# A two-layer decoder trunk on one core: second FFN preparation without GpSimd sums, a written order for its last tiles, and two smaller moves

## The chip, the core and the metric

The kernel runs on one core of a Trainium2 chip. A core has TensorE (PE, matrix products and transposes into PSUM), VectorE (DVE), ScalarE (ACT), GpSimd (POOL) and SyncE (SP, which here issues the DMA transfers). Each engine takes its own instructions in order; waits between engines go by semaphores. The metric is the device time of one execution in microseconds, lower is better.

## The reference

Two residual layers work on x of 1024 tokens x 1024 features in float32. Layer 0 mixes tokens by gMLP and by dilated attention (8 heads, three dilations), layer 1 by chunked gated linear attention (GLA). Each layer then has a gated FFN with a causal convolution of width 3 and 2816 hidden features. Cut to what matters here:

```python
for layer in range(2):
    h = rms_norm(x, norm_mix_g[layer])
    x = x + (even_mixer if layer % 2 == 0 else gla_mixer)(h, ...)   # ends in cat @ w_out
    h = rms_norm(x, norm_ffn_g[layer])
    x = x + conv_ffn(h, ...)

def conv_ffn(h, w_gate, w_up, conv_w, conv_b, w_down):
    g = causal_dwconv(h @ w_gate, conv_w, conv_b)
    return (silu(g) * (h @ w_up)) @ w_down
# attention: the branches of different dilation are weighted by a softmax over their log-denominators and summed
```

## The kernel before, in words

A matrix product takes each float32 operand in two parts: a rounded one (`split`: ScalarE casts it, L108) and the remainder (VectorE subtracts, L109), and does three passes over them. In the rows the parts carry their tile's name, such as `hq` (turned activations), `wo` (out projection), `da` and `dw` (FFN down). A scheduler lists the instructions of each engine in an order of its own, by its own estimates; `tc.keep_in_program_order(ins)` pins an instruction behind the pinned one traced ahead of it on its engine.

Attention runs head pair by head pair (four pairs). A slot of the main loop takes one tile n = 0..7 of a pair: scores, softmax rows, transposes into `pP`, a copy to `pT` (L828, VectorE for even tiles, ScalarE for odd ones), and products into `po`. While pair p runs, the near and the far branch of pair p - 1 are combined (`combine`, `combined`, L941 to L968): group 0 (four token tiles) in slot 4, group 1 in slot 5. A combination takes small operations on `cM`, `cE`, `cD`, one multiplication of `ot` on GpSimd, one of `on` on VectorE (both L964), and an addition (L966).

After the mixer comes the out projection, in column halves: `out_first` makes columns 0 to 511 of all tiles, `out_second` columns 512 to 1023 and, tile by tile, the norm and the transposes for the FFN. The FFN products are done as seven half-size products (p = 1 to 7) on sums of blocks. `first_sides` makes the weight sums for the first feature block while `out_first` runs: for "g" and for "u" it loads two tiles `qg`/`qu`, makes four sums `qS` (p = 5, 6, 7, 3; L249, GpSimd), splits them into `qw` and stores them. `out_second` takes the tiles in the order 0, 4, 1, 5, 2, 3, 6, 7; a tile n >= 4 is combined with tile n - 4 (`second`): four sums `tf..0` to `tf..3`, of which the parts go to `T3[0]`, `T3[1]`, `T3[2]` (rows `T`) and `hq`. The sums t3 and t4 are on GpSimd, except t3 of tile 7. `out_half` runs TensorE's 24 matmuls of a tile (`po1n`, L210) with the transposes of an earlier tile (`pt`, L164) put between them. Tile 7's part (`norm_last`) is handed to `ffn_up` as `norm_end` and stands among its first products `pgB`, `puB`, `puA`, `pgA`; the ones on `T3` are `pgC`, `puC`.

`ffn_down` takes seven products in chunks of two feature pairs: for each, SyncE loads activations `ar` and weights `wr`, which are split into `da` and `dw`; the products go to banks `pdB`, `pdC` (p = 1), `pdO`, `pdP`, `pdQ` (p = 2) and so on. Ahead of all chunks it loads the residual rows `xs[n]` (rows `xr`, eight of 512 KB, L408).

Of the kernel before, what the change touches and what calls it, by code (L numbers as in the profile page):

```python
# [10 lines left out]
F32 = mybir.dt.float32  # L11
# [51 lines left out]
def trunk(ctx: ExitStack, tc: tile.TileContext, a, out):  # L63
# [174 lines left out]
    def first_sides(l, pool, bufs):  # L238

        for kind in "gu":  # L240
# [6 lines left out]
            def summed(p, x, y, op):  # L247
                made[p] = pool.tile([P, 512], F32, tag="qS", bufs=2, name=f"qS{l}{kind}{p}")
                G.tensor_tensor(made[p], x, y, op=op)  # L249
                return made[p]  # L250
# [155 lines left out]
    def ffn_down(l, ps, pool, xs, final):  # L406
        for n in range(NT):
            Q.dma_start(xs[n], xd[l][n])  # L408

# [18 lines left out]
        for p, b, half, c in ((1, "B", 0, 0), (2, "O", 0, 0), (6, "B", 1, 0), (5, "O", 1, 1), (7, "B", 1, 1),  # L428
# [3 lines left out]
            for i, fps in enumerate(CHUNKS):  # L432
                late = p == 4 and fps[0] >= FP // 2 * 2 - TAIL
                both = sides(p, i, pool, tag="tail", bufs=2 * TAIL + 2) if late else sides(p, i)
                if late:
# [62 lines left out]
    def out_second(l, w, x_in, T3, ps, pool):  # L498
# [17 lines left out]

        def second(n, turn, k, b):
            last = n == 7
            gains = gT[:, 0:KD:2, None].to_broadcast([P, 4, P])

            def put(g, pt):
                if last and g == 0:
                    V.tensor_tensor(b[:, g], pt, gains, op=ALU.mult)
                    return
                for j in range(4):
                    A.mul(b[:, g, j, :], pt[:, j, :], gT[:, 2 * j + g : 2 * j + g + 1])

            turn(put, True)
            E = V if last else G
            t1, t2, t3, t4 = (F4(pool.tile([P, 512], F32, tag="S", bufs=4, name=f"tf{n}{i}")) for i in range(4))  # L530
            V.tensor_tensor(t1, b[:, 0], k[:, 0], op=ALU.subtract)
            split(place(T3[0], n), t1)
            V.tensor_tensor(t2, b[:, 1], t1, op=ALU.subtract)
            split(place(T3[1], n), t2)
            E.tensor_tensor(t3, b[:, 1], b[:, 0], op=ALU.subtract)
            split(place(T3[2], n), t3)
            G.tensor_tensor(t4, k[:, 1], t2, op=ALU.subtract)
# [3 lines left out]
        def norm_last(n, xt, ps, junk, h):  # L541

            early = squares(f"{n}a", xt[:, :512], junk[:, :512])
            G.tensor_scalar(early, early, EPS * D, None, op0=ALU.add)

            def rest():
                r = squares(f"{n}b", xt[:, 512:], junk[:, 512:])
                G.tensor_scalar(r, r, early, 1.0 / D, op0=ALU.add, op1=ALU.mult)
                G.tensor_tensor(r, r, mhalf[:, :1], op=ALU.pow)
                for _, c in HALVES:  # L550
                    V.tensor_scalar(h[:, c], xt[:, c], r, None, op0=ALU.mult)
# [969 lines left out]
```

## Time and profile before

| | |
|---|---|
| median of three runs | 2138.92 us (2138.76 to 2140.26) |
| the profiled execution | 2138.33 us |
| its span | 2136.6 us |
| TensorE busy | 2115.9 us (99% of the span), 20.7 us idle |
| VectorE, ScalarE, GpSimd busy | 71%, 48%, 24% |
| granted TensorE clock | 1.000 |
| DMA | 358.66 MB, mean 168 GB/s |

A timeline row gives the start and the length in us, the engine, the line, the operation, the tile written and those read (buffer numbers left out), and in brackets the idle time of the engine just before and what ended it. An "x11" joins instructions that follow one another. A row of the view of waits gives the engine and tile that waited, what it waited for, the total in us, how often, and the longest. The busy time of TensorE includes matmuls that follow one another more slowly than usual.

### The profile page before, as it was taken

The numbers are of one execution on the slowest core, as the hardware profiler recorded it, in microseconds if no ns is written. First come the engines' busy times: TensorE is split into PE (matmuls) and PEld (weight loads), VectorE is DVE, ScalarE is ACT, GpSimd is POOL, SyncE is SP. The second block draws the span as 40 slices with busy tenths as digits, with TensorE's granted clock in tenths as the row PEclk, the third lists the DMA queues.
The fourth block names the chain that finished last, engine by engine and source line by source line (L and its number), as shares of the span: only waits on it lengthen the run. The fifth ranks groups of instructions, "written<-read, shape, count | busy, mean of one in ns | idle before, by whom it ended". The sixth has DMA issues, their size and how long they took to land.

```text
span 2136.6 us, 29596 instructions
## 1 busy us (share of the span) xinstructions
PE 2115.9 (99%) x10380; PEld 1794.7 (84%) x10380; DVE 1514.2 (71%) x2398; ACT 1035.0 (48%) x2008; POOL 523.4 (24%) x553
## 2 busy tenths in 40 slices
PE   8999999999999999999999999999999999999999
PEld 8999988878888888878899888888788888888887
DVE  7466664586878888565576877686788889785554
ACT  7555563365444444344454455545544444444443
POOL 6344311133425344000010011032334334220000
PEclk9999999999999999999999999999999999999999
DMA  7122314854444444755553232396554544458564
GB/s 261 45 74 64 105 45 154 297 198 161 156 150 158 167 163 160 263 212 206 208 176 109 82 103 99 113 329 224 201 171 155 176 147 155 163 172 297 210 221 163
DMA packets 161908, 358.66 MB, mean 168 GB/s; under 512 B 17584, under 2 KB 55216, under 8 KB 161376
## 3 DMA queue, kind: packets, MB, share of 16 engines
q1 hardware_dynamic: 161616, 356.66, 49.2%
q8 instruction: 81, 1.33, 0.3%
q14 instruction: 67, 0.55, 0.1%
q10 hardware_dynamic: 144, 0.13, 0.0%
HBM read 244.20 MB, written 111.74 MB: 167 GB/s over the span
## 4 chain that ended last, share of the span: by engine, by line
PE 72%; DVE 3%; ACT 2%; DMA 1%; issue 1%; SPq 0%; POOL 0%; DVEq 0%; ACTq 0%; POOLq 0%
PE puB L312 11%; PE pgB L312 11%; PE pgC L312 6%; PE puC L312 6%; PE pdB L422 5%; PE pdC L422 5%; PE pv L210 4%; PE pdO L422 4%; PE po L210 3%; PE puA L312 3%; PE pgA L312 3%; PE pdP L422 2%; PE pdQ L422 2%; PE pBq L1212 2%; PE pBr L1212 1%
## 5 line engine op out<-in xcount | busy, mean ns | idle before, releaser
L109 DVE TENSOR_TENSOR da<-ar,da 128x512 fp32r<-128x512 f32 x154 | 106.3, 690 | 154.6 <-ACT da L108 154.4
L108 ACT CAST da<-ar 128x512 fp32r<-128x512 f32 x154 | 95.9, 623 | 211.7 <-PE pdC L422 96.4
L210 PE MATMUL po<-wo,hq 128*128 128x512 f32 x768 | 183.1, 394 | 0.5 <-DVE hq L109 0.4
L210 PEld LDWEIGHTS po<-wo,hq 128*128 128x128 f32 x768 | 142.0, 188 | 30.3 <-DVE hq L109 1.1
L210 PE MATMUL pv<-wv,hq 128*128 128x512 f32 (+2 forms) x768 | 142.3, 341 | 0.0
L422 PE MATMUL pdB<-dw,da 128*128 128x512 f32 x528 | 135.4, 390 | 1.3 <-ACT dw L108 1.3
L422 PE MATMUL pdC<-dw,da 128*128 128x512 f32 x528 | 135.1, 390 | 0.0
L210 PEld LDWEIGHTS pv<-wv,hq 128*128 128x128 f32 x768 | 118.6, 189 | 14.4
L210 PE MATMUL pj<-wq,hq 128*128 128x384 f32 x576 | 120.6, 343 | 0.0
L422 PEld LDWEIGHTS pdB<-dw,da 128*128 128x128 f32 x528 | 98.8, 188 | 22.3 <-ACT dw L108 1.7
L422 PEld LDWEIGHTS pdC<-dw,da 128*128 128x128 f32 x528 | 99.1, 188 | 20.5
L278 POOL TENSOR_TENSOR S1g<-rg 128x512 f32<-128x512 f32 x20 | 29.6, 1481 | 352.0 <-DMA wsd<-D 183.3
L109 DVE TENSOR_TENSOR dw<-wr,dw 128x512 fp32r<-128x512 f32 x154 | 105.8, 687 | 10.5 <-ACT dw L108 9.9
L422 PE MATMUL pdO<-dw,da 128*128 128x512 f32 x396 | 102.2, 389 | 0.2 <-DVE dw L109 0.2
L108 ACT CAST dw<-wr 128x512 fp32r<-128x512 f32 x154 | 95.0, 617 | 11.6 <-DMA wr<-in_w_dn 8.2
L210 PEld LDWEIGHTS pj<-wq,hq 128*128 128x128 f32 x576 | 97.0, 188 | 0.0
L422 PEld LDWEIGHTS pdO<-dw,da 128*128 128x128 f32 x396 | 74.3, 188 | 15.9 <-DVE dw L109 0.6
L153 POOL TENSOR_SCALAR rn<-ssq 128x1 f32<-128x1 f32 x22 | 6.1, 278 | 325.9 <-ACT h L173 244.9
L343 DVE SCALAR_TENSOR_TENSOR t<-g,cw,t 128x1022 f32<-128x1022 f32 x44 | 73.8, 1676 | 0.1
L342 DVE SCALAR_TENSOR_TENSOR t<-g,cw,t 128x1023 f32<-128x1023 f32 x44 | 59.3, 1349 | 16.3 <-ACT t L341 16.3
L327 DVE TENSOR_TENSOR g<-g,s1g 128x512 f32<-128x512 f32 x22 | 15.2, 693 | 78.1 <-ACT s1g L326 78.1
L278 POOL TENSOR_TENSOR S4u<-ru,S2u 128x512 f32<-128x512 f32 x20 | 48.9, 2444 | 54.6 <-DVE wg2p L109 9.7
(1084 smaller groups left out, 5436.1 us busy)
## 6 DMA issues: line engine op xcount, KB each, us to landing
ar<-actd SPq DMA_DIRECT2D x70, 512.0 KB, 3.6
rd<-in_w_down SPq DMA_DIRECT2D x44, 512.0 KB, 3.7
wsd<-D SPq DMA_DIRECT2D x88, 256.0 KB, 2.4
rg<-in_w_gate SPq DMA_DIRECT2D x40, 512.0 KB, 3.7
ru<-in_w_up SPq DMA_DIRECT2D x40, 512.0 KB, 4.7
wr<-wsd SPq DMA_DIRECT2D x40, 512.0 KB, 4.4
actd<-t SPq DMA_DIRECT2D x66, 256.0 KB, 2.2
wr<-in_w_dn SPq DMA_DIRECT2D x30, 512.0 KB, 5.0
```

Of the source, the lines that this page charges most:

```text
L108: (hi or A.copy)(dst[0], src)
L109: (lo or V.tensor_sub)(dst[1], src, f32(dst[0]))
L153: G.tensor_scalar(r, ssq, 1.0 / n, EPS, op0=ALU.mult, op1=ALU.add)
L210: yield T.matmul(o, L[i], R[jj][:, sl], start=(k == 0 and (ii, jj) == PASSES[0]), stop=(k == nk - 1 and (ii, jj) == PASSES[-1]))
L278: G.tensor_tensor(sums[name], x, y, op=op)
L312: mm = T.matmul(o, L[ii][:, j * P : j * P + P], right[p][:, jj, j, :], skip_group_check=more, start=(not more and j == 0 and (ii, jj) == P ...
L327: V.tensor_add(C22, C22, s1)
L342: V.scalar_tensor_tensor(t[:, 1:], g[:, : S - 1], w(1), t[:, 1:], op0=ALU.mult, op1=ALU.add)
L343: V.scalar_tensor_tensor(t[:, 2:], g[:, : S - 2], w(0), t[:, 2:], op0=ALU.mult, op1=ALU.add)
L422: T.matmul(o, L[ii][:, t * P : t * P + P], R[jj], skip_group_check=more, start=start and not more and (ii, jj) == PASSES[0], stop=stop and ...
L1212: T.matmul(o, L[ii][:, j * P : j * P + P], right[p][:, jj, j, :], skip_group_check=more, start=(not more and j == 0 and (ii, jj) == PASSES ...
```

## The change

Four edits: `combine` for group 1 runs in slot 6 instead of slot 5; the sums of `first_sides` are on VectorE; `out_second` has all its sums on VectorE and its last tiles (2, 3, 6, 7) written out with pinned instructions; and `ffn_down` issues the residual loads between the chunks of p = 1 and p = 2, each before the chunk's own products.

```diff
@@ -246,7 +246,7 @@
 
             def summed(p, x, y, op):
                 made[p] = pool.tile([P, 512], F32, tag="qS", bufs=2, name=f"qS{l}{kind}{p}")
-                G.tensor_tensor(made[p], x, y, op=op)
+                V.tensor_tensor(made[p], x, y, op=op)
                 return made[p]
 
             for p in (5, 6, 7, 3, 4, 1, 2):
@@ -404,9 +404,6 @@
 
 
     def ffn_down(l, ps, pool, xs, final):
-        for n in range(NT):
-            Q.dma_start(xs[n], xd[l][n])
-
         def sides(p, c, pool=None, **tag):
 
             k = len(CHUNKS[c])
@@ -432,6 +429,8 @@
             for i, fps in enumerate(CHUNKS):
                 late = p == 4 and fps[0] >= FP // 2 * 2 - TAIL
                 both = sides(p, i, pool, tag="tail", bufs=2 * TAIL + 2) if late else sides(p, i)
+                if p < 3 and i < 4:
+                    tc.keep_in_program_order(Q.dma_start(xs[4 * p - 4 + i], xd[l][4 * p - 4 + i]))
                 if late:
                     tail += both
                     continue
@@ -514,65 +513,112 @@
 
             turn(put, True)
 
+        pin = tc.keep_in_program_order
+
+        def gained(g, pt, b, hold=lambda ins: ins):
+            for j in range(4):
+                hold(A.mul(b[:, g, j, :], pt[:, j, :], gT[:, 2 * j + g : 2 * j + g + 1]))
+
+        def side(name):
+            return F4(pool.tile([P, 512], F32, tag="S", bufs=4, name=name))
+
+        def parted(dst, src):
+            split(dst, src, lo=lambda o, x, h: pin(V.tensor_sub(o, x, h)))
+
+        def less(o, x, y):
+            return V.tensor_tensor(o, x, y, op=ALU.subtract)
+
         def second(n, turn, k, b):
-            last = n == 7
-            gains = gT[:, 0:KD:2, None].to_broadcast([P, 4, P])
-
-            def put(g, pt):
-                if last and g == 0:
-                    V.tensor_tensor(b[:, g], pt, gains, op=ALU.mult)
-                    return
-                for j in range(4):
-                    A.mul(b[:, g, j, :], pt[:, j, :], gT[:, 2 * j + g : 2 * j + g + 1])
-
-            turn(put, True)
-            E = V if last else G
-            t1, t2, t3, t4 = (F4(pool.tile([P, 512], F32, tag="S", bufs=4, name=f"tf{n}{i}")) for i in range(4))
-            V.tensor_tensor(t1, b[:, 0], k[:, 0], op=ALU.subtract)
+            turn(lambda g, pt: gained(g, pt, b), True)
+            t1, t2, t3, t4 = (side(f"tf{n}{i}") for i in range(4))
+            less(t1, b[:, 0], k[:, 0])
             split(place(T3[0], n), t1)
-            V.tensor_tensor(t2, b[:, 1], t1, op=ALU.subtract)
+            less(t2, b[:, 1], t1)
             split(place(T3[1], n), t2)
-            E.tensor_tensor(t3, b[:, 1], b[:, 0], op=ALU.subtract)
+            less(t3, b[:, 1], b[:, 0])
             split(place(T3[2], n), t3)
-            G.tensor_tensor(t4, k[:, 1], t2, op=ALU.subtract)
+            less(t4, k[:, 1], t2)
             split(place(hq[0][1], n), t4)
             split(place(hq[1][1], n), b[:, 1])
 
-        def norm_last(n, xt, ps, junk, h):
-
-            early = squares(f"{n}a", xt[:, :512], junk[:, :512])
-            G.tensor_scalar(early, early, EPS * D, None, op0=ALU.add)
-
-            def rest():
-                r = squares(f"{n}b", xt[:, 512:], junk[:, 512:])
-                G.tensor_scalar(r, r, early, 1.0 / D, op0=ALU.add, op1=ALU.mult)
-                G.tensor_tensor(r, r, mhalf[:, :1], op=ALU.pow)
-                for _, c in HALVES:
-                    V.tensor_scalar(h[:, c], xt[:, c], r, None, op0=ALU.mult)
-                return turning(n, ps, h)
-
-            return rest
-
-        mine, todo = {}, []
-        for i, pair in enumerate(((0, 4), (1, 5), (2, 3), (6, 7))):
+        mine, todo, hx = {}, [], {}
+
+        def rows_of(n, xt):
+            Q.dma_start(xt[:, :512], xd[l][n][:, :512])
+            Q.dma_start(xt[:, 512:], x_in(n)[:, 512:])
+            mine[n] = temp(f"n{n}")
+            hx[n] = pool.tile([P, S], F32, tag="hx", bufs=2, name=f"hx{n}")
+            return xt, mine[n].rearrange("p g a b -> p (g a b)")
+
+        for i, pair in enumerate(((0, 4), (1, 5), (2, 3))):
             xts = pool.tile([P, 2, S], F32, tag="gu"[i % 2], bufs=1, name=f"xt{l}{i}")
             for j, n in enumerate(pair):
-                xt = xts[:, j]
-                Q.dma_start(xt[:, :512], xd[l][n][:, :512])
-                Q.dma_start(xt[:, 512:], x_in(n)[:, 512:])
-                mine[n] = temp(f"n{n}")
-                junk = mine[n].rearrange("p g a b -> p (g a b)")
-                h = pool.tile([P, S], F32, tag="hx", bufs=2, name=f"hx{n}")
-                if n == 7:
-                    rest = norm_last(n, xt, ps, junk, h)
+                xt, junk = rows_of(n, xts[:, j])
                 out_half(l, 1, wo, n, ps, xt[:, 512:], "m1", todo.pop(0) if len(todo) > 1 else None)
-                turn = rest() if n == 7 else norm(n, xt, ps, junk, h)
+                turn = norm(n, xt, ps, junk, hx[n])
                 if n < 4:
                     todo.append(partial(first, n, turn, mine[n]))
                 else:
                     todo.append(partial(second, n, turn, mine[n - 4], mine[n]))
-        todo.pop(0)()
-        return todo.pop()
+
+        xts = pool.tile([P, 2, S], F32, tag="u", bufs=1, name=f"xt{l}3")
+        (x6, j6), (x7, j7) = (rows_of(6 + j, xts[:, j]) for j in range(2))
+        k2, k3, b6, b7 = (mine[n] for n in (2, 3, 6, 7))
+        out_half(l, 1, wo, 6, ps, x6[:, 512:], "m1", todo.pop(0))
+        r6 = inv_rms(squares(6, x6, j6), 1, D, "rn6")
+        early = squares("7a", x7[:, :512], j7[:, :512])
+        G.tensor_scalar(early, early, EPS * D, None, op0=ALU.add)
+
+        def third(g, pt):
+            pin(V.tensor_tensor(k3[:, g], pt, gT[:, g:KD:2, None].to_broadcast([P, 4, P]), op=ALU.mult))
+            to = place(hq[g][0], 3)
+            pin(A.copy(to[0], k3[:, g]))
+            if g == 0:
+                pin(V.tensor_scalar(hx[6], x6, r6, None, op0=ALU.mult))
+                pin(V.tensor_sub(to[1], k3[:, g], f32(to[0])))
+
+        pin(out_half(l, 1, wo, 7, ps, x7[:, 512:], "m1", lambda: turning(3, ps, hx[3])(third, True)))
+        to = place(hq[1][0], 3)
+        pin(V.tensor_sub(to[1], k3[:, 1], f32(to[0])))
+        r7 = small.tile([P, 1], F32, tag="ssq", name="ssq7b")
+
+        def sixth(g, pt):
+            gained(g, pt, b6, pin)
+            if g == 0:
+                pin(A.activation(j7[:, 512:], x7[:, 512:], AF.Square, accum_out=r7))
+                G.tensor_scalar(r7, r7, early, 1.0 / D, op0=ALU.add, op1=ALU.mult)
+                G.tensor_tensor(r7, r7, mhalf[:, :1], op=ALU.pow)
+
+        turning(6, ps, hx[6])(sixth, True)
+        p1, p3, p2, q1 = (side(f"tf{n}") for n in ("61", "63", "62", "71"))
+        pin(less(p1, b6[:, 0], k2[:, 0]))
+        for _, c in HALVES:
+            pin(V.tensor_scalar(hx[7][:, c], x7[:, c], r7, None, op0=ALU.mult))
+        pin(less(p2, b6[:, 1], p1))
+        pin(less(p3, b6[:, 1], b6[:, 0]))
+        parted(place(T3[0], 6), p1)
+
+        def norm_end():
+            gains = gT[:, 0:KD:2, None].to_broadcast([P, 4, P])
+            turning(7, ps, hx[7])(lambda g, pt: gained(g, pt, b7) if g else
+                                  pin(V.tensor_tensor(b7[:, 0], pt, gains, op=ALU.mult)), True)
+            pin(less(q1, b7[:, 0], k3[:, 0]))
+            parted(place(T3[1], 6), p2)
+            parted(place(T3[0], 7), q1)
+            q2 = side("tf72")
+            pin(less(q2, b7[:, 1], q1))
+            parted(place(T3[2], 6), p3)
+            parted(place(T3[1], 7), q2)
+            q3 = side("tf73")
+            pin(less(q3, b7[:, 1], b7[:, 0]))
+            parted(place(hq[1][1], 6), b6[:, 1])
+            parted(place(T3[2], 7), q3)
+            parted(place(hq[1][1], 7), b7[:, 1])
+            for n, k, t in ((6, k2, p2), (7, k3, q2)):
+                pin(less(t, k[:, 1], t))
+                parted(place(hq[0][1], n), t)
+
+        return norm_end
 
 
     def even(gm_open):
@@ -1037,8 +1083,8 @@
             mix(lambda m: m[0] <= slot + 0.5)
             turn()
             previous = output
-            if kind == "n" and p and n in (4, 5):
-                combine(pairs[p - 1], n - 4)()
+            if kind == "n" and p and n in (4, 6):
+                combine(pairs[p - 1], n // 2 - 2)()
         take(6)
         previous()
         for k, ins in enumerate(stream):
```

The orders of the engines at three places, before and after; the names are tiles with their numbers. First VectorE in pair 1 of attention, before: `pT1n6` is the copy for slot 6, `cE00`/`on00` belong to group 0, `cE01`/`on01` to group 1 of pair 0.

```order
L964 TENSOR_TENSOR on00_1614<-on00_1614,cE00_1875 128x4x128
L958 TENSOR_TENSOR cD01_1954<-cE01_1950,ot0n4_999 128x8
L958 TENSOR_TENSOR cD01_1954<-cE01_1950,on01_1616 128x8
L959 TENSOR_TENSOR cD01_1954<-cD01_1954 128x8
L960 RECIPROCAL cD01_1954<-cD01_1954 128x8
L961 TENSOR_TENSOR cE01_1950<-cE01_1950,cD01_1954 128x16
L964 TENSOR_TENSOR on01_1616<-on01_1616,cE01_1950 128x4x128
L966 TENSOR_TENSOR ot0n0_768<-ot0n0_768,on00_1614 128x4x128
L828 COPY pT1n6_1997<-pP1n6_1992 128x512
```

And after:

```order
L1010 TENSOR_TENSOR on00_1614<-on00_1614,cE00_1875 128x4x128
L851 ISA sm1n61_1957,ot1n4_1826<-sc1n61_1954,mband_303 128x4x64
L851 ISA ot1n4_1826 128x1
L1012 TENSOR_TENSOR ot0n0_768<-ot0n0_768,on00_1614 128x4x128
L874 COPY pT1n6_1981<-pP1n6_1976 128x512
L993 TENSOR_TENSOR cM01_1983<-ot0n4_999,on01_1616 128x8
L851 ISA sm1n70_2002,ot1n4_1826<-sc1n70_1999,mband_303 128x4x64
```

Group 1's small operations and its multiplication of `on01` went from ahead of `pT1n6` to behind it, where they begin with `cM01`; group 0's addition stays ahead of it.

VectorE at the end of `out_second` in layer 1, before: `hx7` is tile 7 normalised, `n7` its turned half, `tf6.` and `tf7.` the sums of tiles 6 and 7, `T10` to `T12` the tiles of `T3`.

```order
L551 TENSOR_SCALAR hx7_14339<-xt13_14282,ssq7b_14386 128x512 x2
L109 TENSOR_TENSOR hq11_88<-n6_14285,hq11_88 128x4x128
L109 TENSOR_TENSOR T11_13914<-tf61_14411,T11_13914 128x4x128
L109 TENSOR_TENSOR T12_13915<-tf62_14412,T12_13915 128x4x128
L109 TENSOR_TENSOR hq01_86<-tf63_14413,hq01_86 128x4x128
L320 TENSOR_TENSOR u0_14434<-s1u0_14435,puA0_14519 128x512
L523 TENSOR_TENSOR n7_14338<-pt70_14468,gT1_13951 128x512
L531 TENSOR_TENSOR tf70_14483<-n7_14338,n3_14211 128x512
L533 TENSOR_TENSOR tf71_14484<-n7_14338,tf70_14483 128x512
L535 TENSOR_TENSOR tf72_14485<-n7_14338 128x512
L109 TENSOR_TENSOR hq11_88<-n7_14338,hq11_88 128x4x128
L109 TENSOR_TENSOR T10_13913<-tf70_14483,T10_13913 128x4x128
```

And after:

```order
L596 TENSOR_SCALAR hx7_14288<-xt13_14280,ssq7b_14384 128x512 x2
L529 TENSOR_TENSOR tf62_14408<-n6_14283,tf61_14406 128x512
L529 TENSOR_TENSOR tf63_14407<-n6_14283 128x512
L526 TENSOR_TENSOR T10_13911<-tf61_14406,T10_13911 128x4x128
L320 TENSOR_TENSOR u0_14423<-s1u0_14424,puA0_14515 128x512
L604 TENSOR_TENSOR n7_14287<-pt70_14457,gT1_13949 128x512
L529 TENSOR_TENSOR tf71_14409<-n7_14287,n3_14209 128x512
L526 TENSOR_TENSOR T11_13912<-tf62_14408,T11_13912 128x4x128
L526 TENSOR_TENSOR T10_13911<-tf71_14409,T10_13911 128x4x128
L529 TENSOR_TENSOR tf72_14477<-n7_14287,tf71_14409 128x512
L526 TENSOR_TENSOR T12_13913<-tf63_14407,T12_13913 128x4x128
L320 TENSOR_TENSOR g0_14421<-s1g0_14422,pgA0_14499 128x512
```

Four remainders of tile 6 (`hq11`, `T11`, `T12`, `hq01`) went from between `hx7` and `n7` to behind `n7`'s sum, or further; two sums (`tf62`, `tf63`) and the remainder for `T10` stand there now, and the remainder of `tf71` for `T10` comes second behind its sum instead of fourth.

SyncE at the first chunks of `ffn_down` in layer 0, before (`ar15` and `wr15` are the last chunk of p = 1, `ar20` and `wr20` the first of p = 2; the last five of the eight residual loads are shown):

```order
L408 DMA xr03_8837<-xd03_92 128x1024
L408 DMA xr04_8838<-xd04_93 128x1024
L408 DMA xr05_8839<-xd05_94 128x1024
L408 DMA xr06_8840<-xd06_95 128x1024
L408 DMA xr07_8841<-xd07_96 128x1024
L123 DMA ar15_9060<-actd015_110 128x512
L123 DMA wr15_9062<-in_w_dn 128x512
L123 DMA ar20_9086<-actd020_111 128x1024
```

And after:

```order
L433 DMA xr02_8834<-xd02_91 128x1024
L433 DMA xr03_8835<-xd03_92 128x1024
L123 DMA ar15_9054<-actd015_110 128x512
L123 DMA wr15_9056<-in_w_dn 128x512
L123 DMA ar20_9080<-actd020_111 128x1024
L123 DMA wr20_9082<-in_w_dn 128x1024
L433 DMA xr04_8836<-xd04_93 128x1024
L123 DMA ar21_9121<-actd021_112 128x1024
```

`ar15` stands behind four residual loads instead of eight; the other four stand one ahead of each of the chunks from `ar21`.

## The prediction

> **What bounds the kernel now.** The page's first block comes first, then the waits of TensorE, then the timelines at each of them.
>
> ```profile
> PE 2115.9 (99%) x10380; PEld 1794.7 (84%) x10380; DVE 1514.2 (71%) x2398; ACT 1035.0 (48%) x2008; POOL 523.4 (24%) x553
> ```
>
> TensorE is busy for 2115.9 of 2136.6 us, and the matmuls are the same in kind and number after the change. So the change can win no more than 20.7 us, and only where TensorE stands still; everything that it takes off or loads onto another engine is worth nothing except there. The view of waits, for TensorE, says where it stands (us in total, times, longest):
>
> ```profile
> PE pgC L312 <- DVE T L109: 2.2, 2, 1.5
> ...
> PE pdB L422 <- ACT dw L108: 1.3, 1, 1.3
> PE po2n L837 <- DVE pT2n L828: 1.1, 1, 1.1
> PE po1n L837 <- DVE pT1n L828: 1.1, 1, 1.1
> ...
> PE po3n L837 <- DVE pT3n L828: 0.4, 1, 0.4
> ```
>
> Four of these five lines are at places that the change touches. They sum to 5.7 us of marked idle time. The true losses are a little larger, since matmuls right behind a wait follow each other more slowly; I take them from start to start, with 0.227 us as the time of one 512-column matmul (six take 1.36 us from 906.15 to 907.51, two rows shown under the fourth part).
>
> **Part 1: the second combination of a pair, one slot later.** VectorE's timeline, TensorE's and GpSimd's, in pair 1:
>
> ```profile
> 132.02 1.10 PE L837 MATMUL po1n<-vN,pT1n 128*128 128x64 f32 x8 [1.07 <-DVE pT1n L828]
> 129.22 0.69 DVE L964 TENSOR_TENSOR on<-on,cE 128x512 f32<-128x512 f32 x1
> 129.83 1.53 DVE L966 TENSOR_TENSOR ot0n<-ot0n,on 128x512 f32<-128x512 f32 x1
> 131.28 0.68 DVE L828 COPY pT1n<-pP1n 128x512 f32<-128x512 f32 x1
> 134.87 0.29 DVE L805 CUSTOM_DVE_ANT_0 sm1d<-sc1d,mboth 128x128 f32<-128x128 f32 x1 [0.72 <-PE sc1d L800]
> 129.26 1.55 POOL L964 TENSOR_TENSOR ot0n<-ot0n,cE 128x512 f32<-128x512 f32 x1 [0.82 <-DVE cE L961]
> ```
>
> The copy pT1n at 131.28 is what TensorE waits for. Ahead of it stand the second combination's multiplication (0.69) and the first one's addition, which takes 1.53 beside GpSimd's multiplication (129.26 to 130.81) instead of the 0.69 of its neighbour. In the new order only the first combination's addition is ahead of the copy; the second combination's five small operations, its multiplication and the partner's slowdown come behind. That is at least 0.69 + (1.53 - 0.69) = 1.53 us earlier for the copy, against 1.07 of wait: the wait goes. What then is late? About 2.3 us of work (0.69, 0.69 and the small ones) stand behind the copy, and VectorE has 0.72 us idle at 134.87, so it runs up to 1.6 us behind at that place, where the dilated units begin; their smaller scores leave it room. I cost that at nothing; if the cover is gone it costs up to 1.07 again. Pair 2 repeats it (1.1). Pair 3 does not, by the order: there the copy pT3n stands behind weight preparation, and the rows ahead of it are the same before and after, so its 0.4 stays. Gain: 1.07 + 1.10, rounded up to 2.3 for the slow restart; bounds 0 and 2.5.
>
> **Part 2: the sums of the first FFN sides on VectorE.** Eight sums in each layer go from GpSimd to VectorE.
>
> ```profile
> 362.68 0.62 ACT L108 CAST qw0g<-qS0g 128x512 fp32r<-128x512 f32 x1 [3.75 <-POOL qS0g L249]
> 363.21 0.62 ACT L108 CAST wo<-wo03r 128x512 fp32r<-128x512 f32 x1
> 363.88 0.50 PE L210 MATMUL po<-wo,hq 128*128 128x512 f32 x1 [0.15 <-ACT wo L108]
> 391.60 0.69 DVE L460 TENSOR_TENSOR xh<-xh,po 128x512 f32<-128x512 f32 x1 [2.61 <-PE po L210]
> 395.91 1.28 DVE L109 TENSOR_TENSOR hq<-pc,hq 128x512 fp32r<-128x512 f32 x2
> 393.47 5.72 PE L210 MATMUL po<-wo,hq 128*128 128x512 f32 x24
> 392.78 1.28 POOL L249 TENSOR_TENSOR qS0u<-qu 128x512 f32<-128x512 f32 x1 [14.10 <-DMA qu<-in_w_up]
> ```
>
> ScalarE stood 3.75 us for GpSimd's first sum and only then cast wo03, for which TensorE waited 0.15. In the new order the cast of qw0g5 comes behind both casts of wo03, so that wait goes: 0.3 with the restart, bounds -1 and 0.4. The price is 8 x 0.69 = 5.5 us of VectorE per layer, over eight tiles of TensorE with a pause like the 2.61 before 391.60 in each. A new wait arises: VectorE works in order, and its first sum of the second weight now stands behind the addition of 391.60 (ends 392.29) while the load was there only at about 392.7, when GpSimd started: 0.5 us of standing, with the remainders of tile 6 (395.91 to 397.19 now) queued behind it. Tile 4's product ends at 391.6; one tile more is 24 x 0.227 and eight transposes, some 6.2 us, so TensorE wants them at 397.8. In the new order only two sums and none of the side's remainders are ahead of them, and ScalarE's casts of tile 6 no longer stand behind qw0u: they end near 396.1, with 1.7 us to spare. I take nothing.
>
> **Part 3: the second half of the out projection.** The end of layer 0:
>
> ```profile
> 457.70 0.76 DVE L179 TENSOR_SCALAR hx<-xt,rn 128x1024 f32<-128x1024 f32 x1 [2.13 <-POOL rn L154]
> 463.11 1.93 DVE L551 TENSOR_SCALAR hx<-xt,ssq7b 128x512 f32<-128x512 f32 x2 [0.82 <-POOL ssq7b L549]
> 466.16 1.77 DVE L109 TENSOR_TENSOR hq<-n,hq 128x512 fp32r<-128x512 f32 x1
> 469.67 0.67 DVE L523 TENSOR_TENSOR n<-pt,gT 128x512 f32<-128x512 f32 x1
> 463.06 1.30 POOL L535 TENSOR_TENSOR tf<-n 128x512 f32<-128x512 f32 x1
> 467.49 1.03 PE L164 MATMUL pt<-ident,hx 128*128 128x128 f32 x8
> 472.01 0.39 PE L312 MATMUL pgC<-T,wg0p 128*128 128x512 f32 x1
> 474.22 2.79 PE L312 MATMUL pgC<-T,wg0p 128*128 128x512 f32 x11 [0.66 <-DVE T L109]
> ```
>
> TensorE starts three matmuls at 472.01 and goes on at 474.22: 2.21 - 3 x 0.227 = 1.53 us lost, to the T of the last tile. Its chain: transposes at 467.49 to 468.5, multiplication at 469.67, difference, T. The multiplication came 1.2 us after the transposes because VectorE was behind: the two halves of hx7 took 1.93 beside GpSimd's sum, where one whole tile took 0.76 (457.70), the hq at 466.16 took 1.77 for some 0.69, and tile 6's five remainders were ahead. In the written order only three 0.69 operations (p2, p3 and one T remainder) stand between hx7 and that multiplication, and GpSimd has no large operation left to slow them. So it starts when the first transposes are there, no later than 468.5, and T is complete after 0.67 + 3 x 0.69 = 2.7 us, by 471.3, ahead of 472.01. Tiles 4 to 6 give VectorE two more sums of 0.69 each, paid by the rows that GpSimd no longer stretches. Gain 1.7 (1.53 and something for an earlier hx6; bounds 0.5 and 2.1).
>
> Layer 1 has the same end, tighter:
>
> ```profile
> 1504.90 2.96 DVE L551 TENSOR_SCALAR hx<-xt,ssq7b 128x512 f32<-128x512 f32 x2
> 1510.79 0.68 DVE L523 TENSOR_TENSOR n<-pt,gT 128x512 f32<-128x512 f32 x1
> 1515.20 0.68 DVE L109 TENSOR_TENSOR T<-tf,T 128x512 fp32r<-128x512 f32 x1
> 1512.91 0.50 PE L312 MATMUL pgC<-T,wg0p 128*128 128x512 f32 x1
> 1515.93 2.79 PE L312 MATMUL pgC<-T,wg0p 128*128 128x512 f32 x11 [1.50 <-DVE T L109]
> ```
>
> Lost here: 3.02 - 4 x 0.227 = 2.11 us. From the multiplication (1510.79) to T (1515.88) it is 5.1 us now, and 2.7 in the written order, where the T remainder no longer stands behind a difference, t3 and a slow hq. With a start near 1510.1 (the row u, which stays ahead, waits for TensorE's puA) T is complete at 1512.8, against TensorE's 1512.91: no margin. And n3's first multiplication (0.68 as in 1510.79) now stands ahead of hx6, for which TensorE's transposes of tile 6 can wait: between 0 and 0.7 us, taken as 0.4, nearer the row. Gain 2.1 - 0.4 = 1.7; bounds 0 and 2.5.
>
> **Part 4: the residual loads of FFN down.** SyncE, ScalarE, TensorE, and a window (PE, PEld, DVE, ACT and POOL busy, clock, DMA share, GB/s):
>
> ```profile
> 890.25 7.62 SPq L408 DMA_DIRECT2D xr<-xd  x8
> 898.86 0.32 SPq L123 DMA_DIRECT2D ar<-actd  x1
> 909.02 0.62 ACT L108 CAST da<-ar 128x512 fp32r<-128x512 f32 x1 [9.69 <-DMA ar<-actd]
> 900.00:902.00 2.00, 2.00 (x10) 1.66 (x9) 0.14 (x1) 0.00 (x0) 0.00 (x0) 1.00 1.03 420
> 906.15 1.52 PE L422 MATMUL pdB<-dw,da 128*128 128x512 f32 x6
> 907.51 1.52 PE L422 MATMUL pdC<-dw,da 128*128 128x512 f32 x6
> 910.33 0.50 PE L422 MATMUL pdB<-dw,da 128*128 128x512 f32 x1 [1.30 <-ACT dw L108]
> 914.46 1.42 PE L422 MATMUL pdO<-dw,da 128*128 128x512 f32 x5 [0.16 <-DVE dw L109]
> ```
>
> Eight loads of 512 KB leave SyncE in one burst; the last chunk's activations are issued only at 898.86 and land at about 908.9, ten microseconds later, with the DMA engines full (share 1.03, 420 GB/s). From 907.51 to 914.46 TensorE does 21 matmuls, 4.77 us of work in 6.95: 2.18 lost. In the new order four loads still go in one burst, then the chunk, then one load ahead of each of the next four chunks. SyncE reaches the chunk after half of 7.62 us, at 894.1, 4.7 us earlier. If landing moves by as much it is at 904.2, and TensorE needs it 1.3 us (909.02 to 910.33) before 908.9: margin 3.4. Each later chunk has one 512 KB load in front, 1.25 us at 420 GB/s. Gain 2.0; bounds 0 and 2.2. Layer 1 has no wait of this kind in the list above: nothing.
>
> The Trainium skill, in "DMA: Bandwidth & Descriptors", section "Queues, rings and completion order", says that each DMA engine takes a queue's descriptors in ring order. The trace agrees with it by the ten microseconds at 898.86. By it what counts for the chunk is the bytes ahead, not the time of issue: four loads fewer, 2.1 MB at 420 GB/s, is 5.0 us, landing near 903.9 and the same 2.0 us; but it makes the burst of four that is left a real rival, which a count by issue alone would not.
>
> **Sum.** 2.3 + 0.3 + 1.7 + 1.7 + 2.0 = 8.0 us off the profiled 2138.33 (span 2136.6): 2130.3. That execution lies 0.6 below the median of the runs, 2138.92; the forecast for the median is 2130.4, 0.4% less. All bounds up give 9.7, that is 2128.6.
>
> **Rivals.** (A) VectorE, with 16 to 24 more large operations, is late at the ends: the margins are 0.7 us in layer 0 and 0.1 in layer 1. If half of both gains stays away and the copy of part 1 meets a new queue, 3 to 4 us are lost of the eight: 2134. For it: VectorE is 71% busy already and does not overtake. Against: its stretched rows (1.93, 2.96, 1.77) shrink. (B) The burst of four still delays the chunk, or the loads in front of the next chunks do: the stall moves to pdO and 1.5 to 2 us stay away: 2132.2. For it: engines at 1.03 share; against: the margin of 3.4. (C) The change does not do what it says where it counts: both ends still wait because the chain transposes, multiplication, difference, cast, T has its own latency; and the combination stalls at the next copy. Only the loads and wo03 gain: 2136, within 0.2% of before. (D) Slower: VectorE stands at the sums of part 2 for a weight load, four places (two weights, two layers). At 392.29 it stands 0.5 us and TensorE has 1.7 to spare. To end above 2143.2 the four have to cost 8.0 + 4.3 = 12.3 us, 3.1 each, so VectorE would have to stand 0.5 + 1.7 + 3.1 = 5.3 us at each; nothing in the change delays the loads so far.
>
> **How the numbers follow.** The forecast as worked out 0.52, A 0.16 (it ends faster in four cases of five), B 0.12 (faster), C 0.13, D 0.07. A measurement of this kernel can tell about 0.2%, 4.3 us, from no change: faster means below 2134.6. Faster is 0.52 + 0.13 + 0.12 = 0.77, same 0.03 + 0.13 = 0.16, slower 0.07. The range goes from 2128.0, all bounds up and 0.6 of scatter, over A and B to 2136.0, where C begins; C's upper half and D, with something below, are the 2 in 10 left out.
>
> **What would show it.** Right: no wait of TensorE on pT1n or pT2n from VectorE, none on wo03, pgC at most 0.5 in total, no pdB on dw, pT3n still 0.4; VectorE's hx7 at about 0.8 for two; the 3.75 before qw0g gone. Wrong: a wait on T, hx or pt above 1 us at the ends, a wait on pdO or pdB near 905 to 915, a new wait on hq around 360 to 400 or 1412 to 1445, or on a pT copy with d in its name.

## The result, and the profile after

The changed kernel takes 2129.14 us (median of six runs, 2127.91 to 2130.43), the kernel before 2139.59 (2137.64 to 2142.77): a ratio of 0.995, with a 95% interval of 0.9938 to 0.9963. That is 0.5% faster, 10.4 us by the medians and 9.4 us by the profiled spans (2136.6 and 2127.2). The forecast was 2130.4.

The first block of the page after, and then the whole view of TensorE's waits:

```profile
PE 2112.6 (99%) x10380; PEld 1795.5 (84%) x10380; DVE 1519.3 (71%) x2428; ACT 1034.8 (49%) x2008; POOL 481.2 (23%) x523
```

```profile
PE pj L210 <- ACT wx L118: 5.9, 1, 5.9
PE pj L210 <- DVE qn L929: 1.8, 1, 1.8
PE pBq L1258 <- ACT oq L1266: 1.5, 2, 0.8
PE pt L164 <- DVE hx L577: 0.4, 1, 0.4
PE po L210 <- DVE hq L109: 0.4, 1, 0.4
PE po3n L883 <- DVE pT3n L874: 0.4, 1, 0.4
PE po1n L883 <- ACT pT1n L874: 0.2, 1, 0.2
```

The same matmuls in the same number; the waits for T (2.2), dw (1.3), pT1n and pT2n (1.1 each) are gone. pT3n's 0.4 stays, and one small wait is new, for hx. TensorE stands still for 14.6 us instead of 20.7, which is 6.1 of the 9.4; the other 3.3 came out of its busy time (2115.9 to 2112.6), that is, out of matmuls that followed one another slowly around the waits.

The two profiles can be laid on one another matmul by matmul, since TensorE's work is the same (some 200 of the 10380 stand in another order). The start of the n-th matmul before, less that of the n-th after, is the lead that the change has won by then. It is flat between the places and rises at them:

| place (time before) | lead won, us | forecast |
|---|---|---|
| pair 1 (130) | 1.37 | 2.3 with pair 2 |
| pair 2 (195) | 1.36 | |
| first FFN sides (364) | 0.71 | 0.3 |
| end of layer 0's second half (460 to 475) | 2.58 | 1.7 |
| FFN down, layer 0 (910) | 2.35 | 2.0 |
| end of layer 1's second half (1500 to 1516) | 1.18 | 1.7 |
| sum from 50 us on | 9.55 | 8.0 |

The same places in the profile after. Pair 1, TensorE and VectorE:

```profile
130.95 1.00 PE L883 MATMUL po1n<-vN,pT1n 128*128 128x64 f32 x8
128.41 0.75 DVE L1012 TENSOR_TENSOR ot0n<-ot0n,on 128x512 f32<-128x512 f32 x1 [0.40 <-POOL ot0n L1010]
129.63 0.69 DVE L874 COPY pT1n<-pP1n 128x512 f32<-128x512 f32 x1 [0.47 <-PE pP1n L872]
133.92 1.16 DVE L1010 TENSOR_TENSOR on<-on,cE 128x512 f32<-128x512 f32 x1
137.19 0.42 DVE L874 COPY pT1d<-pP1d 128x256 f32<-128x256 f32 x1 [0.91 <-PE pP1d L872]
```

The copy now waits for TensorE, not the other way about. The second combination's large rows come at 133.92 and later, and the next copy (137.19) still finds VectorE idle for 0.91: the moved work is covered.

The end of layer 0, VectorE and TensorE:

```profile
459.02 0.88 DVE L596 TENSOR_SCALAR hx<-xt,ssq7b 128x512 f32<-128x512 f32 x2 [1.01 <-POOL ssq7b L590]
464.43 0.69 DVE L604 TENSOR_TENSOR n<-pt,gT 128x512 f32<-128x512 f32 x1 [2.72 <-PE pt L164]
465.77 1.48 DVE L526 TENSOR_TENSOR T<-tf,T 128x512 fp32r<-128x512 f32 x2
467.86 2.88 PE L312 MATMUL pgC<-T,wg0p 128*128 128x512 f32 x12
```

hx7 takes 0.88 for its halves (1.93 before), VectorE stands 2.72 us ahead of tile 7's multiplication where it was behind, and T is complete at 467.25, 0.6 ahead of pgC.

The end of layer 1, the same engines:

```profile
1502.70 0.69 DVE L320 TENSOR_TENSOR u<-s1u,puA 128x512 f32<-128x512 f32 x1 [3.30 <-DMA xd<-xt]
1503.31 0.68 DVE L604 TENSOR_TENSOR n<-pt,gT 128x512 f32<-128x512 f32 x1
1504.63 1.46 DVE L526 TENSOR_TENSOR T<-tf,T 128x512 fp32r<-128x512 f32 x2
1492.05 1.06 PE L164 MATMUL pt<-ident,hx 128*128 128x128 f32 x8 [0.41 <-DVE hx L577]
1506.15 2.79 PE L312 MATMUL pgC<-T,wg0p 128*128 128x512 f32 x11
```

T is complete at 1506.09 and its matmuls start at 1506.15: no margin. The row u ahead of the multiplication is released by a store, not by TensorE.

FFN down in layer 0, SyncE and ScalarE:

```profile
884.46 2.86 SPq L433 DMA_DIRECT2D xr<-xd  x4
888.31 0.32 SPq L123 DMA_DIRECT2D ar<-actd  x1
899.19 0.62 ACT L108 CAST da<-ar 128x512 fp32r<-128x512 f32 x1 [5.67 <-DMA ar<-actd]
```

The chunk still lands 10.8 us after its issue. But it is issued earlier, and TensorE wants it near 903.

### The profile page after: what moved, and what is told of

Its sections match the earlier page's. It is cut to its first block, busy times and chain, and to the rows that moved or that the text cites. A ratio compares the mean times of both kernels' runs of the same rounds, so it can differ in the third digit from the quotient of the medians.

```text
span 2127.2 us, 29561 instructions
## 1 busy us (share of the span) xinstructions
PE 2112.6 (99%) x10380; PEld 1795.5 (84%) x10380; DVE 1519.3 (71%) x2428; ACT 1034.8 (49%) x2008; POOL 481.2 (23%) x523
## 4 chain that ended last, share of the span: by engine, by line
PE 95%; DVE 2%; ACT 2%; issue 1%; DMA 1%; POOL 0%; SPq 0%; DVEq 0%; ACTq 0%
PE pgB L312 11%; PE puB L312 11%; PE po L210 8%; PE pv L210 6%; PE pj L210 6%; PE pgC L312 6%; PE pdC L419 6%; PE pdB L419 6%; PE puC L312 6%; PE pdO L419 4%; PE pgA L312 3%; PE puA L312 3%; PE pdQ L419 2%; PE pdP L419 2%; PE pu L210 2%; PE pBq L1258 2%
```

## The experiments

Each was run beside the kernel before on the same chip. The profiles differ by up to 1.8 us ahead of the first edit (last section), so the tables below count from 50 us on: how many us the kernel loses against the changed one at each place, matmul by matmul, in one profiled execution each ("end 0" and "end 1" are the ends of the second half in layers 0 and 1). A place that a kernel does not touch mostly reads between -0.1 and 0.4. The end of layer 1 reads -0.5 to -0.9 in u1_slot, u4_burst and slot5_v: in the changed kernel's own profile a store was late there, and the row u started 1.19 us after tile 7's transposes (1501.51), against some 0.25 in u4_burst and slot5_v. In u1_slot it was 1.07, so this is not the whole of it. u2_sides and its relatives depart further, which is taken up below. By the timed ratios only u3_second, v_unordered and a3_second stand clear of the changed kernel's interval (0.9938 to 0.9963); the smaller differences rest on the profiles.

**Each part undone.** The slot:

```diff
-            if kind == "n" and p and n in (4, 6):
-                combine(pairs[p - 1], n // 2 - 2)()
+            if kind == "n" and p and n in (4, 5):
+                combine(pairs[p - 1], n - 4)()
```

> The changed kernel with the second combination back in slot 5. Theory (each edit removes its own stall of TensorE, and the gains add): the lead of the changed kernel rose by 1.33 and 1.37 us at the two places, so the span of 2127.2 grows by 2.7 to 2129.9, with TensorE's waits for pT1n and pT2n of 1.1 each back and nothing else changed. Rival (the place only moved the wait to another row, and the lead is from elsewhere): less than 1 us.

The sums of the first FFN sides:

```diff
-                V.tensor_tensor(made[p], x, y, op=op)
+                G.tensor_tensor(made[p], x, y, op=op)
```

> The changed kernel with the eight sums of the first FFN sides back on GpSimd, in both layers. Theory: only layer 0 pays, by the cast of qw0g5 ahead of wo03: 0.4 to 0.7 us, span 2127.6 to 2127.9, TensorE's wait for wo back near 356. Rival A (the sums on VectorE cost TensorE something elsewhere, so undoing them gains): below 2127. Rival B (GpSimd's sums slow VectorE's rows where TensorE waits): over 1 us more.

`out_second` as a whole replaced by that of the kernel before:

> The changed kernel with the second FFN preparation of before (sums t3 and t4 on GpSimd, no written order). Theory: the lead rose by 2.4 to 2.9 us at the end of layer 0 and by 1.3 in layer 1, so the span grows by 3.7 to 4.2, to about 2131.1, with waits for T of 0.7 and 1.5 back and the one for hx (0.41) gone. Rival (the ends are limited by the chain of transposes, multiplication, difference and T itself): under 1 us.

The residual loads:

```diff
+        for n in range(NT):
+            Q.dma_start(xs[n], xd[l][n])
...
-                if p < 3 and i < 4:
-                    tc.keep_in_program_order(Q.dma_start(xs[4 * p - 4 + i], xd[l][4 * p - 4 + i]))
```

> The changed kernel with all eight residual loads ahead of the chunks again. Theory: TensorE's wait for dw of 1.3 near 905 is back, with the last chunk of p = 1 landing ten microseconds after its issue: span 2127.2 + 2.3 = 2129.5, and nothing in layer 1. Rival (the four loads in front of the next chunks cost as much as they save in layer 1 or later): the span grows by less than 1.5.

| undone | ratio to before (95%) | span | pair 1 | pair 2 | sides | end 0 | FFN down | end 1 | sum |
|---|---|---|---|---|---|---|---|---|---|
| u1_slot | 0.9961 (0.9946 to 0.9976) | 2130.9 | 1.37 | 1.37 | -0.01 | 0.19 | 0.00 | -0.53 | 2.41 |
| u2_sides | 0.9952 (0.9935 to 0.9969) | 2128.4 | -0.04 | 0.01 | 0.11 | 1.80 | 0.00 | -1.43 | 0.44 |
| u3_second | 0.9989 (0.998 to 0.9998) | 2136.2 | -0.05 | 0.01 | -0.01 | 6.69 | 0.01 | 1.25 | 7.90 |
| u4_burst | 0.9953 (0.9939 to 0.9968) | 2127.6 | -0.03 | -0.01 | 0.01 | 0.00 | 1.48 | -0.90 | 0.55 |

The slot costs 2.74 at its two places for the 2.7 expected; the span, 2130.9 for 2129.9, has 1.3 more ahead of 50 us. The burst costs 1.5 at its place instead of 2.3: in that run the chunk landed at 902.1, 0.9 us earlier relative to TensorE than in the kernel before. Its span grew by only 0.4, as the rival said, but not for the rival's reason: the difference is the -0.90 at the end of layer 1 and not a cost of the loads in front of later chunks. ScalarE's row and TensorE's wait there:

```profile
902.18 0.62 ACT L108 CAST da<-ar 128x512 fp32r<-128x512 f32 x1 [8.84 <-DMA ar<-actd]
903.50 0.50 PE L422 MATMUL pdB<-dw,da 128*128 128x512 f32 x1 [0.45 <-ACT dw L108]
```

The two others missed. u2_sides lost nothing at its own place (0.11) and 1.8 at a place that its edit does not touch; u3_second lost twice what was expected, though it has exactly the code of before there. The scheduler orders the free rows by its own estimates, and in these kernels the rows stand in another order there. In u2_sides, layer 0, VectorE and TensorE:

```profile
467.32 0.69 DVE L320 TENSOR_TENSOR u<-s1u,puA 128x512 f32<-128x512 f32 x1 [3.97 <-ACT n L520]
467.93 0.68 DVE L604 TENSOR_TENSOR n<-pt,gT 128x512 f32<-128x512 f32 x1
470.04 0.50 PE L312 MATMUL pgC<-T,wg0p 128*128 128x512 f32 x1 [1.16 <-ACT T L108]
```

The row u now stands ahead of tile 7's multiplication, as in layer 1 of the changed kernel, and holds it 3.97 us. The trace names ScalarE's n, which u does not read. What u writes is the buffer that held tiles 6 and 7, and their store was 9.2 us under way (457.87 to about 467.1).

**The late row.** This was tested by laying tiles 6 and 7 into the buffer of g, whose first row comes 4.5 us later (471.83 in u2_sides). "u2_tags" is u2_sides with this edit, "tags" the changed kernel with it, "tags_hx6" has hx6 first as well:

```diff
-            xts = pool.tile([P, 2, S], F32, tag="gu"[i % 2], bufs=1, name=f"xt{l}{i}")
+            xts = pool.tile([P, 2, S], F32, tag="ug"[i % 2], bufs=1, name=f"xt{l}{i}")
...
-        xts = pool.tile([P, 2, S], F32, tag="u", bufs=1, name=f"xt{l}3")
+        xts = pool.tile([P, 2, S], F32, tag="g", bufs=1, name=f"xt{l}3")
```

> u2_sides with the buffers of the last two pairs of tiles swapped: tiles 6 and 7 lie in the buffer that g of the FFN takes over, instead of u. In u2_sides TensorE lost 1.8 us at 470, where VectorE stood 3.97 us at the row u, ahead of tile 7's multiplication. Theory (that row waits for the store of tile 7 from the same buffer, 9.2 us under way behind weight loads): the standing goes, TensorE's wait for T of 1.2 goes, span 2128.4 - 1.8 = 2126.6 or less. Rival (it waits for ScalarE, as the trace names it, or the order alone is to blame): no change, 2128.4, the wait of 1.2 stays.

> The changed kernel with only the buffers of the last two pairs of tiles swapped. Theory: in layer 1 the row u (which stood 3.30 us until a store had landed) comes 0.5 to 0.7 earlier, the gap ahead of pgC closes, 0.3 to 0.5 us less, and TensorE's wait for hx (0.41) stays. Rival (the row was not late by the store): the same span, 2127.2, within 0.1.

In tags_hx6 also:

```diff
+            if g == 0:
+                pin(V.tensor_scalar(hx[6], x6, r6, None, op0=ALU.mult))
             pin(V.tensor_tensor(k3[:, g], pt, gT[:, g:KD:2, None].to_broadcast([P, 4, P]), op=ALU.mult))
...
-                pin(V.tensor_scalar(hx[6], x6, r6, None, op0=ALU.mult))
```

> The changed kernel with the same swap of buffers, and tile 6's scaling hx6 ahead of tile 3's first multiplication. Theory: TensorE's wait for hx (0.41) and the slow start behind it go in layer 1, and the row u no longer holds tile 7's multiplication: 0.8 to 1.3 us less, span 2125.9 to 2126.4. Rival (tile 3's multiplication is then late and its remainders hold the first FFN products): 2127.2 or more, with a wait for hq or T.

| | ratio to before (95%) | span | end 0 | end 1 | sum from 50 us |
|---|---|---|---|---|---|
| u2_sides | 0.9952 (0.9935 to 0.9969) | 2128.4 | 1.80 | -1.43 | 0.44 |
| u2_tags | 0.9952 (0.9937 to 0.9966) | 2127.3 | 0.33 | -1.31 | -0.69 |
| tags | 0.9945 (0.9928 to 0.9961) | 2127.7 | 0.00 | -0.79 | -0.84 |
| tags_hx6 | 0.9953 (0.9937 to 0.997) | 2125.9 | 0.28 | -1.09 | -0.86 |

u2_tags has the same order as u2_sides at that place, u ahead of the multiplication. VectorE:

```profile
465.56 0.69 DVE L320 TENSOR_TENSOR u<-s1u,puA 128x512 f32<-128x512 f32 x1 [2.03 <-issue]
466.17 0.68 DVE L604 TENSOR_TENSOR n<-pt,gT 128x512 f32<-128x512 f32 x1
```

The row comes 1.8 us earlier, TensorE's wait for T is gone and 1.5 of the 1.8 us come back: the buffer and its store were the cause, not the order alone. This rests on one profile of each; the timed ratios of the two are the same. The span expected, 2126.6 or less, was not reached (2127.3): 0.3 of the 1.8 stay at that place, and u2_tags is 0.1 worse than u2_sides at two others. For tags and tags_hx6 the gain at the end of layer 1 (0.8 and 1.1) hardly exceeds what kernels without the edit show there (0.5 to 0.9), so that they beat the changed kernel isn't shown: their profiles are 0.85 better from 50 us on, their timed ratios are the same within the intervals. tags_hx6 has no wait for hx any more, and the lowest span of all, in part by its start at full clock.

**Engine or order.** Two kernels complete the square: the old structure with all sums on VectorE, and the written order with sums on GpSimd.

```diff
 v_unordered, in the second() of before:
-            E = V if last else G
...
-            E.tensor_tensor(t3, b[:, 1], b[:, 0], op=ALU.subtract)
+            V.tensor_tensor(t3, b[:, 1], b[:, 0], op=ALU.subtract)
...
-            G.tensor_tensor(t4, k[:, 1], t2, op=ALU.subtract)
+            V.tensor_tensor(t4, k[:, 1], t2, op=ALU.subtract)
```

> The changed kernel with the second FFN preparation of before, but all its sums on VectorE (no written order). Beside u3_second (2136.2 span, sums on GpSimd, no written order) it tells the engine from the order. Theory engine (GpSimd's sums stretch VectorE's rows and hold ScalarE's casts): most of the 9.0 us comes back, span 2127.5 to 2129.5. Theory order (tile 6's remainders ahead of tile 7's multiplication cost it): span 2132 to 2136, waits for T of over 1 us in both layers.

```diff
 g_ordered:
-        def less(o, x, y):
-            return V.tensor_tensor(o, x, y, op=ALU.subtract)
+        def less(o, x, y, E=V):
+            return E.tensor_tensor(o, x, y, op=ALU.subtract)
...
-            less(t3, b[:, 1], b[:, 0])
+            less(t3, b[:, 1], b[:, 0], G)
...
-            less(t4, k[:, 1], t2)
+            less(t4, k[:, 1], t2, G)
...
-        pin(less(p3, b6[:, 1], b6[:, 0]))
+        pin(less(p3, b6[:, 1], b6[:, 0], G))
...
-                pin(less(t, k[:, 1], t))
+                pin(less(t, k[:, 1], t, G))
```

> The changed kernel with the written order kept, but sums t3 and t4 back on GpSimd (t3 of tile 7 excepted, as before). Theory engine: hx7 slow again (over 1.5 us for two), span 2129 to 2132. Theory order: GpSimd's sums stand behind the rows that matter, span 2127.2 to 2128.2. In layer 0 the row u stands ahead of tile 7's multiplication here and may add about 1.2.

| loss at the two ends | sums on GpSimd | sums on VectorE |
|---|---|---|
| no written order | u3_second 6.69 and 1.25 (span 2136.2) | v_unordered 1.34 and 4.72 (span 2134.4; ratio 0.9975, 0.9966 to 0.9985) |
| written order | g_ordered 0.67 and -0.03 (span 2129.0; ratio 0.9957, 0.9942 to 0.9972) | changed kernel 0 and 0 (span 2127.2) |

At the end of layer 0 either one alone takes back most of the 6.69: the order leaves 0.67, the engine 1.34, and neither kernel waits for T there. At the end of layer 1 the order takes back the 1.25 (against the kernels that read -0.5 to -0.9 there, the engine is still worth 0.5 to 0.9), while the engine alone loses 4.72. So the written order wins on either engine, and with it the engine is worth 0.7 us at the two ends, 1.5 at most; without it, moving the sums recovers 1.9 of 7.9. GpSimd does slow VectorE: hx7 in g_ordered takes 1.97 us again, and the rest of its span (2129.0, where the engine theory began) is 1.1 us lost ahead of 50 us.

```profile
461.09 1.97 DVE L596 TENSOR_SCALAR hx<-xt,ssq7b 128x512 f32<-128x512 f32 x2 [1.01 <-POOL ssq7b L590]
```

But that is off the path where the written rows behind it are few. Neither theory fits v_unordered: its span lies in the range of the order theory, but the waits for T of over 1 us in both layers did not come. TensorE's longest waits there, after the ones ahead of 50 us and for oq:

```profile
PE puA L312 <- DMA wu0p<-sided1u: 2.1, 1, 2.1
PE pgC L312 <- DVE T L109: 1.4, 1, 1.4
PE puB L312 <- DMA wu0p<-sided0u: 0.7, 1, 0.7
```

T is waited for in layer 1 alone (1.4, and 0.4 more for ScalarE's part). The longest wait is for a weight load, which is needed earlier in this kernel: the scheduler puts the first matmul of puA third among the first FFN products, where the changed kernel has it 25th. So a good part of the 4.72 seems to come from TensorE's order, not VectorE's; what VectorE's order alone is worth in layer 1, no run separates. u3_second and v_unordered also pay for their pauses a second time (last section).

**Part 3 alone on the kernel before.** `out_second` of the changed kernel in the kernel before, nothing else:

> The kernel before with the new second FFN preparation alone. Theory (the scheduler's free rows decide beside the written ones): in its order the row u stands ahead of tile 7's multiplication in both layers, so layer 0 wins 0.5 to 1.2 instead of 2.5, layer 1 wins 1.3 to 2: span 2136.6 - 2.5 = 2134, with a wait for T of about 1 left in layer 0. Rival (the edits add, as their undoing would say): 7 to 9 us less, 2128 to 2130.

Ratio 0.9976 (0.9967 to 0.9986), span 2133.5. Against before it won 2.15 us at the end of layer 0 and 2.41 in layer 1. Both theories missed: the edit is worth 4.6 at the two ends, neither the 2.5 of a row u that holds tile 7 nor the 8 of the undoing, and no wait for T is left. The row u did stand ahead of the multiplication in layer 0, but here the store had landed in time:

```profile
469.25 0.69 DVE L320 TENSOR_TENSOR u<-s1u,puA 128x512 f32<-128x512 f32 x1 [2.59 <-PE pt L164]
```

This kernel keeps the burst and loses 0.60 us more by it than the kernel before (wait for dw of 1.9 instead of 1.3). At the first FFN sides, with GpSimd's sums, it loses nothing.

**Queue or contention in the slot.** The second combination back in slot 5, GpSimd's part of its group 1 on VectorE:

```diff
-            for i, eng in ((0, G), (1, V)):
+            for i, eng in ((0, V if g else G), (1, V)):
```

> The changed kernel with the second combination in slot 5 as before, and the multiplication of its group 1 that was on GpSimd on VectorE too. Theory queue (the copy pT waits for the rows that stand ahead of it): those rows take 3 x 0.69 = 2.07 instead of 0.69 + 1.53 = 2.22, so waits of about 0.9 for pT1n and pT2n stay, 2.3 us over the changed kernel. Theory contention (GpSimd beside VectorE makes the addition slow, and that is the wait): the addition takes 0.69, waits under 0.3, within 0.5 us of the changed kernel.

Waits of 0.9 and 0.8; 2.76 us lost in the two pairs; ratio 0.9962 (0.9949 to 0.9975), span 2131.3. VectorE:

```profile
131.18 0.69 DVE L1010 TENSOR_TENSOR ot0n<-ot0n,cE 128x512 f32<-128x512 f32 x1
131.79 0.68 DVE L1010 TENSOR_TENSOR on<-on,cE 128x512 f32<-128x512 f32 x1
132.39 0.68 DVE L1012 TENSOR_TENSOR ot0n<-ot0n,on 128x512 f32<-128x512 f32 x1
132.99 0.68 DVE L874 COPY pT1n<-pP1n 128x512 f32<-128x512 f32 x1
```

The addition takes 0.68 instead of 1.53, and TensorE still waits 0.9 instead of 1.1, as the queue theory had it: what stands ahead of the copy counts by its sum, 2.05 us here and 2.22 with GpSimd beside it. The run does not show that the slow addition cost nothing, since a row of 0.69 took the place of the 0.84 that it was longer; it shows that taking GpSimd away is no cure while the rows stay ahead.

## Why the prediction was right, point by point

- **The bound** holds as a total, 9.4 of 20.7. Of that, 6.1 was standing time and 3.3 slow matmuls around it, so "only where TensorE stands still" is too narrow. VectorE has 5 us more work (1514.2 to 1519.3), and all that shows of it on TensorE is the wait of 0.41 for hx.
- **Part 1** was right in mechanism and too small: 2.73 (2.74 by undoing it) for 2.3. The term went by the marked idle time, 1.07 + 1.10, with 0.1 for the slow restart; from start to start it is 1.37 a place. The cover named for the moved rows is there (VectorE idle 0.91 ahead of pT1d).
- **Part 2** won nothing that can be shown. The lead rose by 0.71 there, but u2_sides and a3_second have the sums on GpSimd, with the cast of qw0g5 still ahead of wo03 and standing 3 us, and TensorE loses 0.1 and 0.0. The difference is when a load landed: GpSimd's first sum, released by a load in all three, came some 0.7 us later against TensorE's matmuls in the kernel before. That 0.3 was forecast and 0.71 seen is luck. That the new waits of VectorE cost nothing at this place is right. The prediction did not ask what else these sums move: in layer 1 the kernels with these sums on GpSimd (u2_sides, u2_tags, a3_second) have no wait for hx and stand some 0.5 us better at the end than those with the same code there, since the scheduler orders the matmuls around tile 6's transposes otherwise. So this part may have cost as much as it seemed to win.
- **Part 3, layer 0** was right in its chain (hx7 at 0.88 for the 0.8 put, T complete 0.6 ahead for the 0.7) and too small, 2.58 for 1.7, or 2.15 by a3_second: of the slow start at 458 to 461, where the lead rises by about 0.9, it took in 0.2.
- **Part 3, layer 1**: T at the very start of its matmuls (0.06 for the 0.1 put), hx's wait 0.41 for the 0.4 put. The gain in the profile was 1.18 for 1.7, while u1_slot, u4_burst and slot5_v, which have the same code there, stand at 0.5 to 0.9 less, so 1.7 to 2.1. The one step here that was wrong is the sentence that u "waits for TensorE's puA": it waits for the store too, and u2_sides and u2_tags show what that can cost (1.5 us in layer 0).
- **Part 4** was right: 2.35 for 2.0 (1.48 by undoing it), landing at 904.9 in before's time (899.1 and the lead of 5.8) for 904.2. The landing moved by 4.0 us, and by about 3 against u4_burst, less than the 4.7 of a count by issue. From issue to landing the chunk took 10.1 us before and 10.8 after, so with four loads fewer ahead it was no quicker; it came earlier because it was issued earlier. The Trainium skill ("DMA: Bandwidth & Descriptors", "Queues, rings and completion order") has descriptors taken in ring order. Counting the bytes ahead by that gave an estimate of 5.0 us, which these runs do not bear out.
- **Rivals**: A's margins were as thin as it said (0.6 and 0.06), but the 3 to 4 us were not lost; in u2_sides a late store took 1.8. B, C and D did not come. The total, 9.55 for 8.0 in the profile, is made of four terms that came out larger than forecast, one of them by luck, and one that came out smaller.

## What to carry to other kernels

Where the engine that bounds is 99% busy, list its pauses, trace each to the row it waits for, and look at what stands ahead of that row on its engine; moving that away is worth the pause from start to start, not the marked idle time. In this kernel the written order did more than the change of engine, and the two together the most. An engine in order can be held by a row that nothing waits for yet: a buffer taken over from a tile whose store is still under way does so, and it does not show until a scheduler puts it ahead of something urgent. Where a scheduler has the rest, undoing one edit measures that edit and perhaps a new order elsewhere, so read the lead place by place, not the total.

## What was not expected of the hardware

A pause can cost twice. In u3_second TensorE stood 1.76 and 1.51 us within 5 us, and the granted clock then fell for 4 us:

```profile
471.85 0.50 PE L312 MATMUL pgC<-T,wg0p 128*128 128x512 f32 x1 [1.76 <-ACT T L108]
474.77 4.39 PE L312 MATMUL pgC<-T,wg0p 128*128 128x512 f32 x11 [1.51 <-DVE T L109]
```

Windows of that run (the length of the window, then TensorE, its loads, VectorE, ScalarE, GpSimd busy, clock, DMA share, GB/s), then of v_unordered after one pause of 2.09 us:

```profile
473.00:475.00 2.00, 0.49 (x3) 0.23 (x2) 2.00 (x3) 0.70 (x2) 0.57 (x1) 1.00 0.01 2
475.00:477.00 2.00, 2.00 (x6) 1.57 (x6) 2.00 (x4) 0.00 (x0) 0.00 (x0) 0.56 0.00 0
477.00:479.00 2.00, 2.00 (x7) 1.54 (x6) 1.93 (x4) 0.00 (x0) 0.23 (x1) 0.58 0.56 209
479.00:481.00 2.00, 2.00 (x10) 1.68 (x9) 0.67 (x1) 1.10 (x2) 1.92 (x2) 1.00 1.01 244
```

```profile
1498.00:1500.00 2.00, 2.00 (x8) 1.54 (x8) 1.86 (x4) 1.49 (x3) 1.81 (x2) 0.72 0.91 330
1500.00:1502.00 2.00, 2.00 (x6) 1.54 (x5) 1.68 (x4) 0.16 (x1) 0.29 (x1) 0.50 0.82 328
```

In u3_second the eleven matmuls from 474.77 to 479.00 took 4.2 us instead of 2.5. The kernel before paused 1.50 us at 1515 and kept its clock. The pause for qn near 37 us, which every kernel here has and no edit touches, shows that the length alone doesn't decide. The windows behind it, in the changed kernel (pause 1.82), u3_second (1.81) and u4_burst (2.01):

```profile
38.00:40.00 2.00, 2.00 (x15) 1.96 (x14) 0.85 (x2) 1.34 (x3) 1.78 (x7) 1.00 0.75 228
```

```profile
37.01 1.48 PE L210 MATMUL pj<-wx,hq 128*128 128x384 f32 x7 [1.81 <-DVE qn L882]
38.00:40.00 2.00, 2.00 (x10) 1.97 (x9) 0.95 (x2) 0.89 (x3) 1.78 (x6) 0.59 0.87 257
40.00:42.00 2.00, 2.00 (x10) 1.90 (x10) 0.06 (x1) 0.37 (x1) 1.84 (x4) 0.56 0.07 22
```

```profile
37.33 1.47 PE L210 MATMUL pj<-wx,hq 128*128 128x384 f32 x7 [2.01 <-DVE qn L930]
38.00:40.00 2.00, 2.00 (x15) 1.97 (x14) 0.95 (x2) 1.26 (x3) 1.78 (x8) 1.00 0.87 277
```

In nine of the eleven experiments' profiles TensorE ran at about half clock for 4 us there and lost some 1.5 us against the changed kernel's profile; that is why the tables above start at 50 us. The six runs of the changed kernel spread by 2.5 us, so one or two such falls would do; the untraced runs do not show it. How a pause must fall to be followed by one, no run here settles.
